# The last weight load cut into 16 loads of 8 partitions, and a new order of the last matmuls

## The chip, the core and the metric

The kernel runs on one core of a Trainium2 chip. The metric is the device time of one execution in microseconds; the median of the runs shown is what kernels are compared by. Engines: PE (TensorE) multiplies, DVE (VectorE) and ACT (ScalarE) do the elementwise work, SP (SyncE) issues the DMAs. All tensors are float32.

## What is computed

Two transformer blocks on 256 tokens of width 1024. Only the end matters here: the second block's mixture of experts and the final norm. Each of 16 experts takes 32 tokens (`cap`), chosen by the router:

```python
def expert(args):
    xe, wgu, wd = args
    gu = jnp.einsum('bcd,df->bcf', xe, wgu)
    ga, up = jnp.split(gu, 2, axis=-1)
    return jnp.einsum('bcf,fd->bcd', jax.nn.silu(ga) * up, wd)
ys = lax.map(expert, (jnp.swapaxes(xs, 0, 1), w_gu, w_down))
ys = jnp.swapaxes(ys, 0, 1) * gates[..., None].astype(ys.dtype)
return jax.vmap(lambda ib, yb: jnp.zeros((n, d), yb.dtype).at[ib.reshape(-1)].add(yb.reshape(-1, d)))(idx, ys)
...
x = x + ec_moe(rmsnorm_2(x, norm_ffn_g[layer]), router_w[layer], expert_w_gu[layer], expert_w_down[layer])
return rmsnorm_2(x, final_norm_g)
```

Each expert has weights of 1024x4096 (`w_gu`, 16 MB) and 2048x1024 (`w_down`, 8 MB): 384 MB in all, each byte used once.

## The kernel before, in words

`moe()` loops over the experts `e`. For one expert the `w_gu` load gives G and U (L1327), `silu(G)*U` is transposed to `aT` (L1359), `down` multiplies it by `w_down` (L1366 to L1371) and `scatter` (L1384 to L1394) copies the product out of PSUM and adds it, through a one-hot matrix with the gates in it (`ogT`), to four accumulators `acc[2*t + n]`: `t` is the half of the tokens, `n` the left or right 512 columns. Weights pass through large tiles named `eraw`; all loads are issued by SP, in program order.

The last expert (`e == 15`) is written out at L1416 to L1447. Its `w_down` comes in four parts `raws[0]` to `raws[3]` of 512 rows, four rows to a partition. Parts 0 to 2 are one load each (L1428, 2 MB). Part 3 comes as two loads of 1 MB, left columns and right columns (L1433), each over 128 partitions with four runs of 2 KB. The block under `self.strict()` (L1435 on) keeps PE, ACT and DVE in the written order: down left, scatter left, squares and gain of left; the same for right; then `rstd_q` (L257 to L272, a chain of small DVE and ACT steps on one column) turns the two sums of squares of each token half into a factor; then the scaling (L1445, L1446) and the two stores (L1447).

The order of DMAs on SP: each DMA from SP takes one of eight completion counters in turn (`DMAHW0` to `DMAHW7` in the listings below), so a DMA shares its counter with the one eight DMAs before it and, where that one isn't known to have landed, waits for it. SP issues in order: a DMA that waits holds back all behind it.

Of the kernel before, what the change touches and what calls it, by code (L numbers as in the profile page):

```python
# [9 lines left out]
F32 = mybir.dt.float32  # L10
# [3 lines left out]
AF = mybir.ActivationFunctionType  # L14
OP = mybir.AluOpType
# [4 lines left out]
D = 1024  # L20
# [12 lines left out]
class Body:  # L33
# [1177 lines left out]
    def moe(self):  # L1211
        tc, nc, a = self.tc, self.nc, self.a
        NE, CAP = 16, 32
        wgu, wdn = a["expert_w_gu_2"][0], a["expert_w_down_2"][0]
        with ExitStack() as es:
            ep, x = self.ep, self.x
            ewst = ExitStack()
            ew = self.open("ew", 1, ewst)
# [9 lines left out]
            def slot(n=4096):  # L1228
                pool, tag, bufs = slots[n_unit[0] % len(slots)]
                n_unit[0] += 1  # L1230
                return pool.tile([128, n], F32, name="eraw", tag=tag, bufs=bufs)
# [10 lines left out]
            for t in range(2):  # L1242
                l, r = self.logits[t][:, 0:NE], self.r4[t]
# [8 lines left out]
            p = self.ps()  # L1252
# [14 lines left out]
            p = self.ps()  # L1267
# [8 lines left out]
            acc = [self.ps("acc") for _ in range(4)]  # L1276
            for e in range(NE):
                q = e % 4
                wide = 4 <= e < NE - 1
                if e == 4:  # L1280
# [4 lines left out]
                    ew = self.open("ew4", 1, ewst)  # L1285
# [46 lines left out]
                p = self.ps()  # L1332
                for j in range(4):
                    for t in range(2):
                        nc.tensor.matmul(p[32 * j:32 * j + 32, 256:257], OH[:, t, e, :], self.rc[:, t:t + 1],  # L1335
                                         start=t == 0, stop=t == 1, tile_position=(0, 32 * j))
# [7 lines left out]
                ogT = ew.tile([128, 256], F32, name="ogT", tag="ogT")  # L1344
# [4 lines left out]
                p = self.ps()  # L1349
                if wide:  # L1350

                    idn = self.ident.rearrange("p (a b c) -> p a b c", a=2, b=2)
                    for i in range(8):
                        for b in range(2):
                            nc.tensor.matmul(p[64 * b:64 * b + 64, 64 * i:64 * i + 64], s[:, i:512:8], idn[:, :, b, :],  # L1355
                                             start=True, stop=True, tile_position=(0, 64 * b))
# [7 lines left out]
                y = {0: self.ps(), 512: self.ps()}  # L1364

                def down(j, raw, c0, n):  # L1366

                    for c in range(4):
                        o = 1024 * c + c0
                        nc.tensor.matmul(y[c0][32 * c:32 * c + 32, 0:n], aT[:, c, 32 * j:32 * j + 32],  # L1370
                                         raw[:, o:o + n], start=j == 0, stop=j == 3, tile_position=(0, 32 * c))  # L1371
# [8 lines left out]
                def rows(j):  # L1380
                    return wdn[e, 512 * j:512 * j + 512].rearrange("(p i) n -> p i n", i=4)


                def scatter(c0, n, out, first):  # L1384
                    ys = ew.tile([128, n], F32, name="ys", tag="ys")
                    if e == NE - 1 and c0:
                        nc.vector.tensor_copy(ys[:, 0:256], y[c0][:, 0:256])
                        nc.scalar.activation(ys[:, 256:512], y[c0][:, 256:512], AF.Copy)
                    elif c0 == 0:
                        nc.scalar.activation(ys, y[c0][:, 0:n], AF.Copy)  # L1390
                    else:
                        nc.vector.tensor_copy(ys, y[c0][:, 0:n])  # L1392
                    for t in range(2):
                        nc.tensor.matmul(out[t], ogT[:, t * 128:(t + 1) * 128], ys, start=first, stop=e == NE - 1)  # L1394

                if wide:
                    for j in range(2):
# [8 lines left out]
                if e < NE - 1:  # L1406
                    for n in range(2):
                        scatter(512 * n, 512, acc[n::2], e == 0)
                if e == 3:

                    for t in range(2):
                        for n in range(2):
                            nc.tensor.matmul(acc[2 * t + n], self.ident, x[:, t, 512 * n:512 * n + 512],  # L1413
                                             start=False, stop=False)

            end = e_[1][0].tile([128, 8192], F32, name="eraw", tag="e")  # L1416
            grow, g, junk = end[0:1, 0:D], end[:, D:2 * D], end[:, 2 * D:2 * D + 512]
            nc.sync.dma_start(grow, a["final_norm_g_2"].rearrange("(o d) -> o d", o=1))
            for n in range(2):
                p = self.ps()  # L1420
                nc.tensor.matmul(p, self.ones[0:1, :], grow[:, 512 * n:512 * n + 512], start=True, stop=True)
                nc.scalar.activation(g[:, 512 * n:512 * n + 512], p, AF.Copy)
            fo = end[:, 4 * D:6 * D].rearrange("p (t n) -> p t n", t=2)
            with self.queued([silu]):
                nc.scalar.activation(fo[:, 0, 0:1], self.eps, AF.Sqrt)
            raws = [w[:, o:o + 4096] for w in (slot(8192), slot(8192)) for o in (0, 4096)]
            for j in range(3):
                nc.sync.dma_start(raws[j], rows(j).rearrange("p i n -> p (i n)"))  # L1428
                for n in range(2):
                    down(j, raws[j], 512 * n, 512)  # L1430
            for n in range(2):
                c = slice(512 * n, 512 * n + 512)
                nc.sync.dma_start(raws[3].rearrange("p (i n) -> p i n", i=4)[:, :, c], rows(3)[:, :, c])  # L1433
            ss = [self.small.tile([128, 16], F32, name="ss", tag="st1", bufs=4) for _ in range(2)]
            with self.strict():  # L1435
                for n in range(2):
                    c = slice(512 * n, 512 * n + 512)
                    down(3, raws[3], 512 * n, 512)
                    scatter(512 * n, 512, acc[n::2], False)
                    for t in range(2):  # L1440
                        nc.scalar.activation(junk, acc[2 * t + n], AF.Square, accum_out=ss[t][:, n:n + 1])
                        nc.vector.tensor_tensor(fo[:, t, c], acc[2 * t + n], g[:, c], OP.mult)
                r = self.rstd_q(*ss)
                for t in range(2):
                    nc.scalar.activation(fo[:, t, 0:512], fo[:, t, 0:512], AF.Copy, scale=r[t])  # L1445
                    nc.vector.tensor_scalar(fo[:, t, 512:D], fo[:, t, 512:D], r[t], None, OP.mult)  # L1446
                    nc.sync.dma_start(self.out[t * 128:(t + 1) * 128, :], fo[:, t, :])  # L1447
            self.close(est, ewst, self.bigst)


# [44 lines left out]
```

## Time and profile before

| | us |
|---|---|
| median of 3 runs | 1509.54 |
| the runs | 1507.14, 1509.54, 1552.52 |
| the profiled execution, its own time | 1507.54 |
| its span, first to last instruction | 1505.8 |
| time outside the span | 1.7 |

In the page's 40 slices the DMA row stands at 9 from slice 19 on: over the experts the 16 DMA engines are the busy resource, and PE, at 6 tenths, waits for weights. In the last slices the loads run out and the chain passes to PE, ACT and DVE. Times in the timeline are microseconds from the start of the span; the number behind the start is the duration, and in square brackets stands how long the engine was idle before and what ended it.

### The profile page before, as it was taken

Reading aid. Unit: us, or ns where it says so; the run is one execution under the profiler, and the core shown is the slowest. Engines: PE = TensorE matmul, PEld = TensorE weight load, DVE = VectorE, ACT = ScalarE, POOL = GpSimd, SP = SyncE. Lnnn points to the kernel's source line nnn. Section 1 sums busy time; section 2 is a strip of 40 time slices with the busy share of each in tenths; the row PEclk is TensorE's granted clock in tenths of the full one; section 3 lists DMA queues with packets and bytes.
Section 4 is the critical chain, followed back from the end, with each engine's and each line's share of the span. In section 5 each row is a group of like instructions: output and inputs, shape, how many; then the busy total and the mean of one; then the engine's idle time right before and its main releaser. Section 6 shows DMA issues by size and latency. Waiting matters only on the chain.

```text
span 1505.8 us, 18173 instructions
## 1 busy us (share of the span) xinstructions
PE 1176.1 (78%) x7948; PEld 699.6 (46%) x7948; DVE 418.1 (28%) x786; ACT 356.7 (24%) x611; POOL 7.0 (0%) x19
## 2 busy tenths in 40 slices
PE   7999999999999999885676756666656666566665
PEld 5988989999978775321121211212211113112111
DVE  6844667455578855100000000000000000000001
ACT  5554556344466633000000000000000000000002
POOL 1000000000000000000000000000000000000000
PEclk9999999999999999998787788878878789778788
DMA  9754447555633289999999999999999999999995
GB/s 302 231 168 149 160 146 261 188 190 196 206 102 127 87 318 424 403 427 429 433 430 431 430 430 430 430 430 430 431 431 431 431 431 431 430 431 430 430 429 236
DMA packets 93054, 503.00 MB, mean 334 GB/s; under 512 B 7707, under 2 KB 60207, under 8 KB 78512
## 3 DMA queue, kind: packets, MB, share of 16 engines
q1 hardware_dynamic: 92976, 501.85, 82.8%
q8 instruction: 62, 1.02, 0.3%
q14 instruction: 16, 0.13, 0.0%
HBM read 500.79 MB, written 1.05 MB: 333 GB/s over the span
## 4 chain that ended last, share of the span: by engine, by line
PE 34%; another core or an unknown queue 15%; DMA 8%; DVE 2%; issue 1%; ACT 1%; SPq 0%; DVEq 0%; ACTq 0%
PE sm L1327 18%; DMA eraw<-in_expert_w_down_dram 8%; PE sm L1377 7%; PE acc L1394 4%; PE sm L1370 2%; PE sm L1355 2%; PE sm L1297 1%; DVE es L1348 1%; DVE ys L1392 1%; PE sm L1343 0%; ACT aT L1361 0%; PE acc L1413 0%; PE sm L1335 0%; DVE rsl L1338 0%
## 5 line engine op out<-in xcount | busy, mean ns | idle before, releaser
L1327 PE MATMUL sm<-eraw,xs 128*32 128x512 f32 x2048 | 318.5, 778 | 187.6 <-DMA eraw<-in_expert_w_gu_dram 187.6
L1327 PEld LDWEIGHTS sm<-eraw,xs 128*32 128x32 f32 x2048 | 75.0, 137 | 412.9 <-DMA eraw<-in_expert_w_gu_dram 211.3
L74 DVE TENSOR_TENSOR whl<-raw,whl 128x1024 fp32r<-128x1024 f32 x152 | 181.7, 1220 | 102.8 <-ACT whl L73 101.7
L73 ACT ACTIVATE whl<-raw 128x1024 fp32r<-128x1024 f32 x152 | 154.2, 1053 | 77.0 <-issue 46.0
L1377 PE MATMUL sm<-eraw,aT 128*32 128x512 f32 x704 | 106.5, 760 | 63.5 <-DMA eraw<-in_expert_w_down_dram 59.4
L1348 DVE SCALAR_TENSOR_TENSOR es<-sm,rsl,es 128x512 f32<-128x512 f32 x16 | 12.0, 750 | 443.6 <-PE sm L1327 440.7
L1347 ACT ACTIVATE es<-sm,rsl 128x512 f32<-128x512 f32 x16 | 11.0, 687 | 411.2 <-PE sm L1327 411.2
L127 PE MATMUL acc<-xh,whl 128*128 128x256 f32 x704 | 93.2, 280 | 0.0
L127 PE MATMUL sm<-xh,whl 128*128 128x256 f32 x704 | 89.7, 280 | 0.0
L1377 PEld LDWEIGHTS sm<-eraw,aT 128*32 128x32 f32 x704 | 26.1, 135 | 133.4 <-issue 62.8
L127 PEld LDWEIGHTS sm<-xh,whl 128*128 128x128 f32 x704 | 86.1, 189 | 0.7
L127 PEld LDWEIGHTS acc<-xh,whl 128*128 128x128 f32 x704 | 85.5, 188 | 1.1
L1392 DVE COPY ys<-sm 128x512 f32<-128x512 f32 x15 | 10.4, 691 | 236.5 <-PE acc L1394 236.5
L1394 PE MATMUL acc<-ys,ogT 128*128 128x512 f32 x128 | 64.3, 625 | 14.0 <-DVE ys L1392 11.9
L127 PE MATMUL acc<-whl,xh 128*128 128x512 f32 x240 | 65.4, 403 | 0.2
L1390 ACT ACTIVATE ys<-sm 128x512 f32<-128x512 f32 x16 | 9.6, 597 | 202.0 <-PE sm L1377 147.5
L1370 PE MATMUL sm<-eraw,aT 128*32 128x512 f32 x320 | 45.8, 710 | 13.8 <-DMA eraw<-in_expert_w_down_dram 10.7
L127 PE MATMUL acc<-whl,aH 128*128 128x512 f32 x176 | 55.7, 389 | 0.0
L1345 ACT ACTIVATE ogT<-sm 128x256 f32<-128x256 f32 x16 | 6.1, 383 | 195.2 <-PE sm L1343 195.2
L1394 PEld LDWEIGHTS acc<-ys,ogT 128*128 128x128 f32 x128 | 22.1, 193 | 58.8 <-issue 25.6
L127 PEld LDWEIGHTS acc<-whl,xh 128*128 128x128 f32 x240 | 44.4, 190 | 10.4 <-ACT xh L162 0.8
L127 PE MATMUL acc<-xl,whl 128*128 128x256 f32 x352 | 48.5, 278 | 0.0
(399 smaller groups left out, 1255.6 us busy)
## 6 DMA issues: line engine op xcount, KB each, us to landing
eraw<-in_expert_w_gu_dram SPq DMA_DIRECT2D x56, 4096.0 KB, 53.2
eraw<-in_expert_w_down_dram SPq DMA_DIRECT2D x22, 4096.0 KB, 53.0
eraw<-in_expert_w_down_dram SPq DMA_DIRECT2D x19, 2048.0 KB, 30.9
raw<-in_w_in_dram SPq DMA_DIRECT2D x34, 1024.0 KB, 5.4
eraw<-in_expert_w_gu_dram SPq DMA_DIRECT2D x16, 2048.0 KB, 17.3
raw<-in_w_gate_dram SPq DMA_DIRECT2D x11, 1024.0 KB, 5.4
raw<-in_w_up_dram SPq DMA_DIRECT2D x11, 1024.0 KB, 5.4
raw<-in_w_down_dram SPq DMA_DIRECT2D x11, 1024.0 KB, 4.9
```

What stands on the lines that cost most here:

```text
L73: nc.scalar.activation(H[:, k], raw[:, k], AF.Copy)
L74: self.at["L"] = nc.vector.tensor_tensor(L[:, k], raw[:, k], H[:, k].bitcast(F32), OP.subtract).ins
L127: nc.tensor.matmul(out, l[i], r[j], start=first and p == 0 and q == 0, stop=last and p == 2 and q == n - 1)
L1297: nc.tensor.matmul(pg[kk][:, i * 128:(i + 1) * 128], x[:, t, feats(k)], OH[:, t, e:e + 4, :].rearrange("p e s -> p (e s)"), start=t == 0, ...
L1327: nc.tensor.matmul(dst[32 * j:32 * j + 32, :], xs[:, k, 32 * q:32 * q + 32], raw[:, o + 512 * j:o + 512 * j + 512], start=k == 0, stop=k = ...
L1347: silu = nc.scalar.activation(s, G, AF.Silu, scale=rs).ins
L1348: nc.vector.scalar_tensor_tensor(s, U, rs, s, OP.mult, OP.mult)
L1355: nc.tensor.matmul(p[64 * b:64 * b + 64, 64 * i:64 * i + 64], s[:, i:512:8], idn[:, :, b, :], start=True, stop=True, tile_position=(0, 64 ...
L1370: nc.tensor.matmul(y[c0][32 * c:32 * c + 32, 0:n], aT[:, c, 32 * j:32 * j + 32], raw[:, o:o + n], start=j == 0, stop=j == 3, tile_position ...
L1377: nc.tensor.matmul(y[c0][32 * c:32 * c + 32, :], aT[:, i, j, :], raw[:, o:o + 512], start=j == 0 and i < 4, stop=j == 1 and i >= 4, tile_p ...
L1392: nc.vector.tensor_copy(ys, y[c0][:, 0:n])
L1394: nc.tensor.matmul(out[t], ogT[:, t * 128:(t + 1) * 128], ys, start=first, stop=e == NE - 1)
```

## The change

`raws[3]`'s right half is loaded by 16 DMAs of 8 partitions each instead of one of 128. The right columns of `down` become two groups of 256 columns, at 512 and at 768, in two PSUM banks, for all four parts. In the last block `down` of both halves stands ahead of the left scatter; the right half is copied out of PSUM by DVE (columns 512 on) and ACT (768 on) into `yr`, and its scatter is two matmuls of 256 columns for each token half. The gain of the last accumulator (`acc[3]`) is no longer a step of its own: it is done with the factor in one instruction at the end. Both stores are outside the strict block.

```diff
                 def scatter(c0, n, out, first):
                     ys = ew.tile([128, n], F32, name="ys", tag="ys")
-                    if e == NE - 1 and c0:
-                        nc.vector.tensor_copy(ys[:, 0:256], y[c0][:, 0:256])
-                        nc.scalar.activation(ys[:, 256:512], y[c0][:, 256:512], AF.Copy)
-                    elif c0 == 0:
+                    if c0 == 0:
                         nc.scalar.activation(ys, y[c0][:, 0:n], AF.Copy)
                     else:
                         nc.vector.tensor_copy(ys, y[c0][:, 0:n])
                     for t in range(2):
-                        nc.tensor.matmul(out[t], ogT[:, t * 128:(t + 1) * 128], ys, start=first, stop=e == NE - 1)
+                        nc.tensor.matmul(out[t], ogT[:, t * 128:(t + 1) * 128], ys, start=first, stop=False)
...
+            y[768] = self.ps()
             for j in range(3):
                 nc.sync.dma_start(raws[j], rows(j).rearrange("p i n -> p (i n)"))
-                for n in range(2):
-                    down(j, raws[j], 512 * n, 512)
+                for c0, n in ((0, 512), (512, 256), (768, 256)):
+                    down(j, raws[j], c0, n)
             for n in range(2):
                 c = slice(512 * n, 512 * n + 512)
-                nc.sync.dma_start(raws[3].rearrange("p (i n) -> p i n", i=4)[:, :, c], rows(3)[:, :, c])
+
+                for o in range(0, 128, 8) if n else (0,):
+                    i = slice(o, o + (8 if n else 128))
+                    nc.sync.dma_start(raws[3].rearrange("p (i n) -> p i n", i=4)[i, :, c], rows(3)[i, :, c])
             ss = [self.small.tile([128, 16], F32, name="ss", tag="st1", bufs=4) for _ in range(2)]
             with self.strict():
+                down(3, raws[3], 0, 512)
+                yl = ew.tile([128, 512], F32, name="ys", tag="ys")
+                nc.scalar.activation(yl, y[0], AF.Copy)
+                for c0 in (512, 768):
+                    down(3, raws[3], c0, 256)
+                yr = ew.tile([128, 2, 256], F32, name="yr", tag="es")
+                nc.vector.tensor_copy(yr[:, 0], y[512][:, 0:256])
+                for t in range(2):
+                    nc.tensor.matmul(acc[2 * t], ogT[:, t * 128:(t + 1) * 128], yl, start=False, stop=True)
+                nc.scalar.activation(yr[:, 1], y[768][:, 0:256], AF.Copy)
                 for n in range(2):
-                    c = slice(512 * n, 512 * n + 512)
-                    down(3, raws[3], 512 * n, 512)
-                    scatter(512 * n, 512, acc[n::2], False)
                     for t in range(2):
+                        if n:
+                            for i in range(2):
+                                nc.tensor.matmul(acc[2 * t + 1][:, 256 * i:256 * i + 256], ogT[:, t * 128:(t + 1) * 128],
+                                                 yr[:, i], start=False, stop=i == 1)
                         nc.scalar.activation(junk, acc[2 * t + n], AF.Square, accum_out=ss[t][:, n:n + 1])
-                        nc.vector.tensor_tensor(fo[:, t, c], acc[2 * t + n], g[:, c], OP.mult)
+                        if n == 0:
+                            nc.vector.tensor_tensor(fo[:, t, 0:512], acc[2 * t], g[:, 0:512], OP.mult)
+                nc.vector.tensor_tensor(fo[:, 0, 512:D], acc[1], g[:, 512:D], OP.mult)
                 r = self.rstd_q(*ss)
                 for t in range(2):
                     nc.scalar.activation(fo[:, t, 0:512], fo[:, t, 0:512], AF.Copy, scale=r[t])
-                    nc.vector.tensor_scalar(fo[:, t, 512:D], fo[:, t, 512:D], r[t], None, OP.mult)
-                    nc.sync.dma_start(self.out[t * 128:(t + 1) * 128, :], fo[:, t, :])
+                nc.vector.tensor_scalar(fo[:, 0, 512:D], fo[:, 0, 512:D], r[0], None, OP.mult)
+                nc.vector.scalar_tensor_tensor(fo[:, 1, 512:D], acc[3], r[1], g[:, 512:D], OP.mult, OP.mult)
+            for t in range(2):
+                nc.sync.dma_start(self.out[t * 128:(t + 1) * 128, :], fo[:, t, :])
```

SP's queue at the end of the program, before. The names in brackets are what the DMA waits for; `DMAHW` is a counter of an earlier DMA.

```order
L1236 DMA eraw<-in_expert_w_gu_dram 128x8192 [waits DMAHW4_49,PE_49]
L1418 DMA eraw<-in_final_norm_g_dram 1x1024 [waits DMAHW7_49,PE_49]
L1428 DMA eraw<-in_expert_w_down_dram 128x4096 [waits DMAHW5_49]
L1428 DMA eraw<-in_expert_w_down_dram 128x4096
L1428 DMA eraw<-in_expert_w_down_dram 128x4096 [waits DMAHW6_49]
L1433 DMA eraw<-in_expert_w_down_dram 128x4x512
L1433 DMA eraw<-in_expert_w_down_dram 128x4x512 [waits DMAHW0_49]
L1447 DMA out_dram<-eraw 128x1024 [waits DMAHW1_49,DVE_49,Activation_49]
L1447 DMA out_dram<-eraw 128x1024 [waits DMAHW2_49,DVE_49,Activation_49]
```

The same place in the changed kernel, from the left half on; of the 16 small loads the counters run from 0 to 7 twice.

```order
L1434 DMA eraw<-in_expert_w_down_dram 128x4x512
L1434 DMA eraw<-in_expert_w_down_dram 8x4x512 [waits DMAHW0_49]
L1434 DMA eraw<-in_expert_w_down_dram 8x4x512 [waits DMAHW1_49]
...
L1434 DMA eraw<-in_expert_w_down_dram 8x4x512 [waits DMAHW6_49]
L1434 DMA eraw<-in_expert_w_down_dram 8x4x512 [waits DMAHW7_49]
L1434 DMA eraw<-in_expert_w_down_dram 8x4x512 [waits DMAHW0_49]
...
L1434 DMA eraw<-in_expert_w_down_dram 8x4x512 [waits DMAHW6_49]
L1434 DMA eraw<-in_expert_w_down_dram 8x4x512 [waits DMAHW7_49]
L1463 DMA out_dram<-eraw 128x1024 [waits DMAHW0_49,DVE_49,Activation_49]
L1463 DMA out_dram<-eraw 128x1024 [waits DMAHW1_49,DVE_49,Activation_49]
```

One load that waited on counter 0 has become 16 that wait on counters 0 to 7 and again 0 to 7. Counter 7 is the left half's; the stores' counters moved from 1 and 2 to 0 and 1.

PE at the end of the program, before (`ys` is the copy of the product, `acc` the accumulators):

```order
L1370 MATMUL sm<-eraw,aT 32x512 [waits DMAHW7_49]
L1370 MATMUL sm<-eraw,aT 32x512 x3
L1394 MATMUL acc<-ys,ogT 128x512 [waits Activation_49]
L1394 MATMUL acc<-ys,ogT 128x512
L1370 MATMUL sm<-eraw,aT 32x512 [waits DMAHW0_49]
L1370 MATMUL sm<-eraw,aT 32x512 x3
```

and the same in the changed kernel:

```order
L1370 MATMUL sm<-eraw,aT 32x512 [waits DMAHW7_49]
L1370 MATMUL sm<-eraw,aT 32x512 x3
L1370 MATMUL sm<-eraw,aT 32x256 [waits DMAHW4_49,DMAHW5_49,DMAHW3_49,DMAHW6_49,DMAHW2_49,DMAHW7_49,DMAHW1_49,DMAHW0_49]
L1370 MATMUL sm<-eraw,aT 32x256 x7
L1445 MATMUL acc<-ys,ogT 128x512 [waits Activation_49]
L1445 MATMUL acc<-ys,ogT 128x512
L1451 MATMUL acc<-yr,ogT 128x256 [waits DVE_49]
L1451 MATMUL acc<-yr,ogT 128x256 [waits Activation_49]
```

The left scatter (L1394, now L1445) stood between the two halves of `down` and now stands behind both, so behind the first matmul of the right half, which waits on all eight counters.

## Rows read from the trace of the kernel before

**Rows 1.** The page's slices: DMA engines' share in tenths, GB/s.

```profile
DMA  9754447555633289999999999999999999999995
GB/s 302 231 168 149 160 146 261 188 190 196 206 102 127 87 318 424 403 427 429 433 430 431 430 430 430 430 430 430 431 431 431 431 431 431 430 431 430 430 429 236
```

**Rows 2.** Timeline, last expert: start, duration, engine, line, operation, idle before.

```profile
1461.58 5.34 PE L1327 MATMUL sm<-eraw,xs 128*32 128x512 f32 x32 [4.16 <-DMA eraw<-in_expert_w_gu_dram]
...
1471.32 6.07 PE L1327 MATMUL sm<-eraw,xs 128*32 128x512 f32 x32 [4.40 <-DMA eraw<-in_expert_w_gu_dram]
...
1477.52 0.75 DVE L1348 SCALAR_TENSOR_TENSOR es<-sm,rsl,es 128x512 f32<-128x512 f32 x1 [31.27 <-PE sm L1327]
...
1486.09 1.92 PE L1370 MATMUL sm<-eraw,aT 128*32 128x512 f32 x16 [1.54 <-DMA eraw<-in_expert_w_down_dram]
...
1488.77 1.06 PE L1370 MATMUL sm<-eraw,aT 128*32 128x512 f32 x8 [0.75 <-DMA eraw<-in_expert_w_down_dram]
...
1490.61 1.98 PE L1394 MATMUL acc<-ys,ogT 128*128 128x512 f32 x4 [0.78 <-ACT ys L1390]
...
1492.52 1.07 PE L1370 MATMUL sm<-eraw,aT 128*32 128x512 f32 x8
...
1494.90 1.98 PE L1394 MATMUL acc<-ys,ogT 128*128 128x512 f32 x4 [1.31 <-ACT ys L1388]
...
1496.98 0.60 ACT L1441 ACTIVATE eraw<-acc 128x512 f32<-128x512 f32 x1 [0.23 <-PE acc L1394]
...
1497.48 0.19 ACT L1441 ACTIVATION_READ_ACCUMULATOR eraw<-acc 128x1 f32 x1
...
1498.31 0.20 DVE L264 TENSOR_SCALAR rstq<-ss 128x1 f32<-128x1 f32 x1
...
1500.06 0.21 DVE L271 TENSOR_SCALAR rstq<-rstq 128x1 f32<-128x1 f32 x1
...
1500.19 0.87 DVE L1446 TENSOR_SCALAR eraw<-eraw,rstq 128x512 f32<-128x512 f32 x2
```

**Rows 3.** The two loads of part 3: issue durations and starts, time to landing.

```profile
L1433 SPq DMA_DIRECT2D eraw<-in_expert_w_down_dram x2: 603/4726/8850, 1447.8 to 1451.8; - x2
...
DMA to landing us min/median/max: 39.5/40.2/40.9
```

**Rows 4.** SP's waits from 1440 us on.

```profile
SPq L1433 <- DMA eraw<-in_expert_w_gu_dram: 3.4, 1, 3.4
```

**Rows 5.** Issues of small loads on SP, by timeline and by line.

```profile
4.12 5.09 SPq L390 DMA_DIRECT2D bf<-in_b_forget_dram  x1
...
408.45 0.36 SPq L759 DMA_DIRECT2D cw<-in_mlstm_conv_w_dram  x1
...
1445.92 0.24 SPq L1418 DMA_DIRECT2D eraw<-in_final_norm_g_dram  x1
...
L771 SPq DMA_DIRECT2D pw<-in_pool_w_dram x4: 486/586/596, 410.8 to 414.0; - x4
...
DMA to landing us min/median/max: 1.9/2.0/3.6
```

**Rows 6.** Busy time by stretch; the last three columns are PEclk, DMA share, GB/s.

```profile
1476.00:1484.00 8.00, 7.06 (x52) 2.28 (x44) 0.75 (x1) 3.96 (x6) 0.00 (x0) 0.98 1.01 412
...
1485.00:1489.00 4.00, 2.15 (x20) 0.57 (x24) 0.00 (x0) 0.00 (x0) 0.00 (x0) 1.00 0.50 186
...
1442.23:1445.87 3.64, 3.64 (x48) 1.41 (x48) 0.00 (x0) 0.00 (x0) 0.00 (x0) 1.00 1.00 428
...
1461.58:1466.92 5.34, 5.34 (x32) 1.26 (x32) 0.00 (x0) 0.00 (x0) 0.00 (x0) 0.68 1.02 436
...
1489.80:1497.00 7.20, 5.00 (x20) 1.51 (x16) 1.93 (x4) 3.06 (x9) 0.00 (x0) 1.00 0.05 20
```

**Rows 7.** DMA packets of the stretch 1485 to 1489.

```profile
q1 hardware_dynamic: 382, 0.74, 49.6%
```

## The prediction

> **What bounds the kernel now.** I read the page's slices first, then the timeline of the last 65 us, then the DMA issues of that stretch. The slices show the DMA engines full from slice 19 on at about 430 GB/s [rows 1]: 384 MB of expert weights set the time, and nothing in the change touches that part. What it can touch is the end, behind the last weight byte.
>
> There the reader is to see three moments. The left half of part 3 was issued at 1447.8 and took 40.9 us to land, so 1488.7; PE starts on it at 1488.77 [rows 2, 3]. The right half was issued at 1451.8 and took 39.5, so 1491.3 [rows 3]. PE starts on it at 1492.52, with no idle time in the row, because it was still at the left scatter, 1490.61 to 1492.59 [rows 2]. So the right half's landing is not on the path: it has 1.2 us to spare. From 1492.52 to the end of the span at 1505.8 are 13.28 us: right down 1.07, a wait for the copies, scatter 1.98 from 1494.90, squares, the factor chain, scaling, stores.
>
> Before 1484 the 16 DMA engines are at share 1.01, from 1485 at 0.50 [rows 6]: half of them have run out of work some 6 us ahead of the others. That is the slack that a different split of the last megabyte could use.
>
> **The change, part by part, against the profiled execution: 1507.54 us, span 1505.8.** That is 2.0 under the median shown (1509.54), and 0.4 above the lowest run.
>
> *The new order behind the landing.* Call t0 the moment at which PE can start the right half's matmuls. Behind it now stand, in PE's order: right down 1.07 (two groups of 256 columns for one of 512, the same columns), left scatter 1.98, right scatter 1.98 [rows 2]; together 5.03. The two copies of the right product lie beside the left scatter now and cost nothing; the cover is 1.98 us of PE, the copies need under 0.5 each. ACT's last square ended 0.79 behind PE's last scatter (1494.90 + 1.98 = 1496.88 to 1497.67): 5.82. DVE's gain of the last accumulator has left this place. The factor chain took from 1498.31 to 1500.27, 1.96 us, of which its first column's steps can start before the last square is done, so that it ends at about t0 + 7.6. The scaling took 0.79 from there to 1501.06 [rows 2]; one of its two instructions (about 0.48, the overlap of the pair taken out) is now a scalar_tensor_tensor that reads PSUM, 0.75 by its row, so 1.06: t0 + 8.7. From there to the end 4.74 as before (1501.06 to 1505.8). Sum: t0 + 13.4, against 13.28 before. The reordering, seen from the right half's start, is worth nothing: what it takes out (waiting copies, one gain) is what it puts in (the left scatter, 1.98, which was done beforehand). It pays only if t0 comes earlier than 1492.52.
>
> *The extra matmuls of parts 0 to 2.* Same columns, twelve more instructions; PE idles 1.54 and 0.75 before the next parts [rows 2], which covers them. Nothing.
>
> *The 16 loads, and what t0 becomes.* The second load of part 3 waited 3.4 us for a w_gu load [rows 4], and 8.85 us more in its issue [rows 3]: that w_gu load is eight DMAs ahead of it, and the listing shows the wait on counter 0. The 16 loads wait in the same way, each for the DMA eight before it. The first seven wait for loads that are needed earlier anyhow (the third w_gu load was there at 1461.58, the last at 1471.32, part 2 at 1486.09 [rows 2]) and are out by then. **The eighth waits on counter 7, and that is the left half, which lands at 1488.7.** SP issues in order, so loads 8 to 16, 9/16 of the right half, cannot be issued before 1488.77, whatever DMA engines stand idle. Load 16 needs counter 7 again: load 8's landing.
>
> The price of such an issue and landing is not in the trace for this shape. Nearest rows: 0.24 (one partition), 0.36 (20 partitions), 0.49 to 0.60 (64 partitions, 16 KB) for an issue, 1.9 to 2.0 for the landing of a small load, 3.6 at worst [rows 5]. I take 0.36 for the issue, whose row is nearest in partitions, 0.05 between two, and 2.0 for the landing. Load 16 is issued eight slots behind load 8: 1488.77 + 8 x 0.41 = 1492.05, and has landed at 1494.05. Load 8 itself lands at 1490.8, so load 16 isn't held by it. So t0 = 1494.05, 1.5 later than PE starts on the right half now, and 4.2 us later than PE is ready for it (1488.77 + 1.06). Ends: 0.24 with 0.04 between and a landing of 1.9 give 1492.9; 0.60 with 0.05 and 2.0 give 1496.0.
>
> *PE's clock in the new gap.* [...] In the trace the 32 matmuls behind a gap of 4.16 took 5.34 us at a mean clock of 0.68, those behind 4.40 took 6.07, and the same kind of work with PE busy ran at 1.00 (3.64 us in the stretch from 1442.23) [rows 2, 6]. So a gap like this cost 1.7 and 2.4; gaps of 1.5 cost nothing. I take 1.7, from the row with the nearest gap; the ends are 0 and 2.4. All of PE's 5.03 us behind t0 is on the path, so it counts in full.
>
> **Sum:** t0 later by 1.5, the tail by 0.1, the clock 1.7: +3.3 to +3.4 us. 1507.54 + 3.4 = **1510.9 us**. Low end of this case: 0.4 + 0.1 = +0.5; high end: 3.5 + 0.1 + 2.4 = +6.0.
>
> **Rivals.**
>
> *A. The balance works.* The 16 loads land by the time the left half's matmuls end (1489.84), because they sit on DMA engines that run out at about 1485. Then t0 = 1489.84, no gap, the end at 1489.84 + 13.4 = 1503.2: 2.6 us less, 1504.9. For it: the share of 0.50 from 1485 on, and 64 packets to an engine are only 64 x 0.083 = 5.3 us (382 packets in 4 us at 49.6% of 16 engines are 83 ns each [rows 7]), which fits between about 1482 and 1489. Against it: the wait on counter 7 in SP's queue, which no faster engine lifts. [...] Chance 0.15.
>
> *B. The issue is dear.* The only load over 8 partitions in the trace, L390, held SP for 5.09 us [rows 5]. At that price the nine late loads take 9 x 5.1 = 46 us, t0 is about 1537 and the kernel 44 us slower, 1552: over 2%. It decides from about 3.5 us an issue on. Against it: L390 reads single elements and is issued 4 us after the start, when SP is just filling the queue, and larger loads there take 0.4 to 0.8; the right half's own 8.85 [rows 3] came with some 15 MB of loads still ahead of it, and at 1489 none is. Chance 0.03.
>
> *C. The clock stays up, or the issues are at the cheap end.* +0.5 to +1.7, 1508.0 to 1509.2. This is the low part of the forecast's range; it shares its 0.70.
>
> The remaining 0.12 is for holds that are shorter than computed and land between A and C, 1505 to 1508.
>
> **How the numbers follow.** Forecast 0.70 (with C), A 0.15, B 0.03, the rest 0.12. The time is the likeliest case's, 1510.9. The range reaches down to A, 1504.9, with 0.4 for the spread to the lowest run, and up to 1507.54 + 6.0 = 1513.5 with 2.0 for the distance of the profiled execution to the median: 1504.5 to 1515.5. A measurement of this kernel can tell about 2%, 30 us, from no change. Only B reaches that: slower 0.03; no mechanism here gains 30 us, faster 0.01; within 2% 0.96.
>
> **What would show it.** In the profile of the changed kernel: the left half's matmuls start near 1488.8 as now; SP's issues of the small loads show seven spread out over 1452 to 1486 and nine in a row from 1488.8 on, at 0.3 to 0.6 each; PE idles about 4 us between the left and the right half of part 3 and names a w_down DMA for it; its clock in the last 12 us is under 1.00; from the right half's start to the end of the span are 13.4 us at full clock, 15 otherwise. Wrong would be: small loads issued in a row before 1488, an idle time of PE there under 1 us (rival A), or single issues of several us after 1488 (rival B). If the tail is 13.4 but t0 is off, the issue price or the landing was mis-sized; if t0 is right and the tail long, the clock.

## The result, and the profile after

| | before | after |
|---|---|---|
| median, us | 1508.76 (4 runs) | 1517.61 (1516.58 to 1517.95, 4 runs) |
| the profiled execution, its span | 1507.54, 1505.8 | 1517.95, 1515.9 |

The ratio is 1.0059, interval 1.0048 to 1.0071: slower by 0.6%, about 9 us, outside the forecast range (1504.5 to 1515.5) on the side that was forecast. One of the runs of before, at 1552.52, was disturbed and is left out of the ratio.

The chain of waits of the changed kernel, from the left half's issue on (start, duration, what):

```profile
1448.72 41.95 DMA eraw<-in_expert_w_down_dram
1490.67 0.02 issue
1490.68 0.67 SPq L1434
1491.36 0.04 issue
1491.40 0.67 SPq L1434
...
1495.69 0.67 SPq L1434
1496.36 0.04 issue
1496.41 4.58 DMA eraw<-in_expert_w_down_dram
1500.99 0.14 issue
1501.13 1.93 PE sm L1370 x16
```

The left half lands at 1490.67, SP issues the eighth small load in the same moment, seven more behind it 0.72 apart, and the last one at 1496.41; that one takes 4.58 us to land. The SPq pieces are the chain: this is the hold on counter 7 that the prediction named. SP's own rows agree. It waits four times for w_down loads, 15.1 us in all. The last of these waits runs from the end of the seventh small load's issue, 1488.55, to the left half's landing. Below: the waits, the seventh issue, and the issues of part 3 (left half and 16 loads: shortest, median and longest issue).

```profile
SPq L1434 <- DMA eraw<-in_expert_w_down_dram: 15.1, 4, 5.7
```

```profile
1487.88 0.67 SPq L1434 DMA_DIRECT2D eraw<-in_expert_w_down_dram  x1
```

```profile
L1434 SPq DMA_DIRECT2D eraw<-in_expert_w_down_dram x17: 613/672/9092, 1448.7 to 1496.4; - x17
```

The timeline of the changed kernel, to be held against [rows 2]:

```profile
1471.70 5.22 PE L1327 MATMUL sm<-eraw,xs 128*32 128x512 f32 x32 [4.76 <-DMA eraw<-in_expert_w_gu_dram]
...
1487.91 4.48 PE L1370 MATMUL sm<-eraw,aT 128*32 128x512 f32 x32 [3.81 <-DMA eraw<-in_expert_w_down_dram]
...
1501.13 1.93 PE L1370 MATMUL sm<-eraw,aT 128*32 128x256 f32 x16 [8.73 <-DMA eraw<-in_expert_w_down_dram]
...
1502.99 3.29 PE L1445 MATMUL acc<-ys,ogT 128*128 128x512 f32 x4
...
1506.12 1.89 PE L1451 MATMUL acc<-yr,ogT 128*128 128x256 f32 x8
...
1510.84 0.75 DVE L1461 SCALAR_TENSOR_TENSOR eraw<-acc,rstq,eraw 128x512 f32<-128x512 f32 x1
```

PE idles 8.73 us ahead of the right half, where 4.2 were forecast, and the left scatter behind it takes 3.29 instead of 1.98. Also part 2 and the left half come later: PE waits 3.81 us for part 2, where it waited 1.54.

Busy time by stretch of the changed kernel (last three columns PEclk, DMA share, GB/s):

```profile
1482.00:1485.00 3.00, 2.10 (x32) 0.77 (x24) 0.00 (x0) 0.00 (x0) 0.00 (x0) 1.00 0.90 277
...
1495.00:1500.00 5.00, 0.00 (x0) 0.00 (x0) 0.00 (x0) 0.00 (x0) 0.00 (x0) 0.54 0.48 66
...
1501.13:1508.01 6.88, 6.88 (x28) 3.35 (x28) 1.85 (x4) 2.45 (x7) 0.00 (x0) 0.67 0.00 0
```

```profile
q1 hardware_dynamic: 207, 0.33, 48.0%
```

The second fence is the DMA packets of 1495 to 1500. The DMA share is 0.48 there and the traffic 66 GB/s; in the kernel before about the same share moved 186 [rows 6]. A packet took 0.48 x 16 x 5 / 207 = 0.185 us, against 0.083 in [rows 7].

At 1482 to 1485 the first small loads run beside parts 2 and 3. There the whole core's traffic is down too, to 277 GB/s. The same stretch of the kernel before:

```profile
1482.00:1485.00 3.00, 2.55 (x24) 0.52 (x16) 0.00 (x0) 0.00 (x0) 0.00 (x0) 1.00 0.97 380
```

Packets of 16 KB belong here to parts 0 to 2 alone. Taken one by one from the trace, they last 0.80 us in the mean in this stretch, 0.64 before. So something slowed the small loads' packets and those of other loads with them. The prediction had no term for that.

### The profile page after: what moved, and what is told of

It reads as the page before. It is cut to its first block, busy times and chain, and to the rows that moved or that the text cites. A ratio compares the mean times of both kernels' runs of the same rounds, so it can differ in the third digit from the quotient of the medians.

```text
span 1515.9 us, 18266 instructions
## 1 busy us (share of the span) xinstructions
PE 1183.0 (78%) x7984; PEld 703.1 (46%) x7984; DVE 417.9 (28%) x785; ACT 356.6 (24%) x611; POOL 7.0 (0%) x19
## 4 chain that ended last, share of the span: by engine, by line
PE 71%; another core or an unknown queue 14%; DMA 9%; DVE 3%; ACT 2%; issue 1%; SPq 1%; DVEq 0%; ACTq 0%
PE acc L127 20%; PE sm L1327 18%; PE sm L127 10%; DMA eraw<-in_expert_w_down_dram 8%; PE sm L1377 7%; PE acc L1391 3%; PE sm L1370 2%; PE sm L1355 2%; PE sm L1297 1%; PE acc L1176 1%; DVE es L1348 1%; DVE ys L1389 1%; PE acc L1208 1%; DMA x<-in_x_dram 0%
## 5 line engine op out<-in xcount | busy, mean ns | idle before, releaser
L1377 PE MATMUL sm<-eraw,aT 128*32 128x512 f32 x704 | 111.9, 794 | 57.9 <-DMA eraw<-in_expert_w_down_dram 54.9
L1391 PE MATMUL acc<-ys,ogT 128*128 128x512 f32 x120 | 59.5, 618 | 11.9 <-DVE ys L1389 11.9
L1370 PE MATMUL sm<-eraw,aT 128*32 128x512 f32 (+1 forms) x352 | 45.7, 664 | 24.9 <-DMA eraw<-in_expert_w_down_dram 22.0
L127 PE MATMUL sm<-xl,whl 128*128 128x256 f32 x352 | 48.3, 280 | 0.0
```

What stands on the lines that cost most here:

```text
L127: nc.tensor.matmul(out, l[i], r[j], start=first and p == 0 and q == 0, stop=last and p == 2 and q == n - 1)
L1377: nc.tensor.matmul(y[c0][32 * c:32 * c + 32, :], aT[:, i, j, :], raw[:, o:o + 512], start=j == 0 and i < 4, stop=j == 1 and i >= 4, tile_p ...
```

## The experiments

Two theories were to be told apart. *Hold*: the small loads that are issued only behind the left half's landing, times the price of an issue, make the loss. *Place*: loads that cover few neighbouring partitions are slow and slow the others. Since kernels reach the end some 1 to 3 us earlier or later for reasons far ahead of it, the table counts from PE's start on the last w_gu load (W), where PE waits for its landing in every kernel.

| right half | W | left half start | right half start | span | right half from W | from there to the end |
|---|---|---|---|---|---|---|
| before: 1 load, old order | 1471.32 | 1488.77 | 1492.52 | 1505.8 | 21.2 | 13.3 |
| after: 16 x 8 neighbours | 1471.70 | (landed 1490.67) | 1501.13 | 1515.9 | 29.4 | 14.8 |
| E1: 1 load, new order | 1470.80 | in one row with part 2 | 1490.84 | 1503.6 | 20.0 | 12.8 |
| E2: 7 loads, neighbours | 1471.00 | 1491.23 | 1494.49 | 1510.0 | 23.5 | 15.5 |
| E3: 8 x 16 neighbours | 1472.74 | in one row with part 2 | 1496.50 | 1510.8 | 23.8 | 14.3 |
| E4: 16 x 8, four apart | 1470.89 | 1488.26 | 1496.62 | 1510.8 | 25.7 | 14.2 |
| E5: 16 x 8 neighbours, old order | 1473.26 | 1492.27 | 1501.47 | 1517.0 | 28.2 | 15.5 |
| E6: 7 loads, eight apart | 1471.08 | 1490.27 | 1494.32 | 1509.5 | 23.2 | 15.2 |
| E7: 16 loads of 128 x 512 B | 1473.67 | in one row with part 2 | 1496.02 (last wait) | 1510.4 | 22.4 | 14.4 |
| E8: 4 x 32, four apart | 1474.19 | 1491.56 | 1494.32 | 1506.9 | 20.1 | 12.6 |
| E9: 4 x 32 neighbours | 1473.10 | 1495.00 | 1497.88 | 1512.0 | 24.8 | 14.1 |

All but E5 have the new order of the matmuls. `i` are the partitions of a load. Each kernel was profiled once. From W to the end the profiles differ from before's 34.5 us as the ratios of the run times do, within 1.8 us (the changed kernel 9.7 more against 8.9, E4 5.4 against 5.9). So a few tenths between two rows of the table are not shown to be real.

### E1: the order alone

```diff
-                for o in range(0, 128, 8) if n else (0,):
-                    i = slice(o, o + (8 if n else 128))
+                for i in (slice(0, 128),):
```

> The new order of the last matmuls with the right half in one load of 128 partitions as before. If the loss is all in the 16 loads: the right half lands near 1491.4 us, PE idles about 1.5 us between the halves of part 3 with its clock at the upper level, and the end comes 13.4 us after that start: span about 1504.9, 1 us under before, ratio 0.999 to 1.000. If the order itself costs (left scatter behind the right half, one more wait): span 1507 or more.

Measured: 1507.09 us, ratio 0.9985 (0.9975 to 0.9994), span 1503.6: 0.15% faster than before, and the only kernel here whose interval lies below 1.

```profile
1490.84 1.07 PE L1370 MATMUL sm<-eraw,aT 128*32 128x256 f32 x16 [0.67 <-DMA eraw<-in_expert_w_down_dram]
1491.84 1.98 PE L1444 MATMUL acc<-ys,ogT 128*128 128x512 f32 x4
1493.66 1.89 PE L1450 MATMUL acc<-yr,ogT 128*128 128x256 f32 x8
```

PE goes through right half and both scatters without a gap, at a granted clock of 1.00 from 1490.84 to 1495.55; the copies lie beside the left scatter. The order gains 1.2 us up to the right half's start and 0.5 behind it. All of the loss is in the 16 loads.

### E5: the loads alone

```diff
-                nc.sync.dma_start(raws[3].rearrange("p (i n) -> p i n", i=4)[:, :, c], rows(3)[:, :, c])
+                for i in [slice(o, o + 8) for o in range(0, 128, 8)] if n else (slice(0, 128),):
+                    nc.sync.dma_start(raws[3].rearrange("p (i n) -> p i n", i=4)[i, :, c], rows(3)[i, :, c])
```

> The kernel before with the 16 loads of 8 neighbouring partitions for the right half and nothing else changed. If the landing sets the end, the old order gives back nothing: the left scatter runs at 1490.6 as before, PE then waits for the right half until about 1501, and from there 13.3 us at full clock, 14.5 to 15 behind the long gap: span 1514.5 to 1516, ratio about 1.005, the changed kernel's. If the new order were a part of the loss: 2 us or more under the changed kernel.

Measured: 1518.91 us, ratio 1.0059 (1.0044 to 1.0074), span 1517.0. From W to the end 43.7 us against 44.2 in the changed kernel, and both have the ratio 1.0059: as expected, the loads alone make the whole loss. The new order's gain of 1.7 us (E1) is gone once the late landing sets the end; the changed kernel, which has that order, is even 0.5 longer from W. The span is 1 us over the expected one, since W is 1.6 later.

### E4: the same 16 loads, their partitions four apart

```diff
-                for o in range(0, 128, 8) if n else (0,):
-                    i = slice(o, o + (8 if n else 128))
+                for i in [slice(32 * b + r, 32 * b + 32, 4) for b in range(4) for r in range(4)] if n else (slice(0, 128),):
```

> The changed kernel with its 16 loads of 8 partitions, each load's partitions four apart instead of neighbours; the counters, the waits, the issues and the bytes are the same. If packets are slow because eight of them go to neighbouring partitions: packets near 87 ns to the end (207 ns in the changed kernel after 1495), no slowdown at 1482 to 1485, left half landed at 1489 instead of 1490.7, last landing about 2.5 us after its issue: PE starts on the right half near 1497, span near 1512, 4 us less. [...]

Measured: 1515.43 us, ratio 1.0039 (1.0025 to 1.0053), span 1510.8. That span is 5 us under the changed kernel's, but the profiled run is the fastest of E4's five; by the ratios the gain is 0.2%, 3 us, and from W to the end it is 4.3. Timeline and two stretches of E4, then the packets of the second stretch:

```profile
1488.26 1.06 PE L1370 MATMUL sm<-eraw,aT 128*32 128x512 f32 x8 [0.72 <-DMA eraw<-in_expert_w_down_dram]
1496.62 1.94 PE L1370 MATMUL sm<-eraw,aT 128*32 128x256 f32 x16 [7.30 <-DMA eraw<-in_expert_w_down_dram]
```

```profile
1482.00:1485.00 3.00, 2.26 (x36) 0.83 (x28) 0.00 (x0) 0.00 (x0) 0.00 (x0) 1.00 0.66 262
...
1490.00:1495.00 5.00, 0.00 (x0) 0.00 (x0) 0.00 (x0) 0.05 (x1) 0.00 (x0) 0.81 0.31 92
```

```profile
q1 hardware_dynamic: 280, 0.46, 31.5%
```

A packet took 0.315 x 16 x 5 / 280 = 0.090 us, near the 0.083 of before, and half of the changed kernel's 0.185 (the expectation's 207 ns is 185 by that row). At 1482 to 1485 a share of 0.66 moved 262 GB/s, where the changed kernel needed 0.90 for 277. The left half came in time, and the right half 3.7 us earlier from W (25.7 against 29.4). The 92 GB/s of the second stretch are what SP issues: 64 KB each 0.72 us. Same loads, same counters, same issues: place costs 3.7 us in these two profiles. What is left, 25.7 against E1's 20.0, is hold: the left half's matmuls start at 1488.26, the right half's 8.4 us behind, while eight issue slots and one landing of 2.5 us go by.

### E7: 16 loads over all partitions

```diff
-                for o in range(0, 128, 8) if n else (0,):
-                    i = slice(o, o + (8 if n else 128))
-                    nc.sync.dma_start(raws[3].rearrange("p (i n) -> p i n", i=4)[i, :, c], rows(3)[i, :, c])
+                for q in [(r, slice(c.start + o, c.start + o + 128)) for r in range(4) for o in range(0, 512, 128)] if n else ((slice(0, 4), c),):
+                    nc.sync.dma_start(raws[3].rearrange("p (i n) -> p i n", i=4)[:, q[0], q[1]], rows(3)[:, q[0], q[1]])
```

> The changed kernel with its 16 loads cut the other way: each over all 128 partitions, one run of 512 B in each (64 KB as before), on the same counters, so that loads 8 to 16 still wait for the left half. Hold theory: nine issues in a row behind 1488.2, each 0.4 (as a load with one run per partition) to 0.7 (as now), landing 2 to 2.5 us behind the last: PE starts on the right half at 1493.7 to 1496.5, span 1507.5 to 1511, 3 to 6 us over the new order with one load, though no packet is slowed by neighbours. If only neighbouring partitions cost: as the new order with one load, 1503.5 to 1505.

Measured: 1511.0 us, ratio 1.0012 (1.0002 to 1.0022), span 1510.4, last wait for the right half over at 22.4 from W. The line of its loads and their time to landing, then its chain from the left half's landing on:

```profile
L1433 SPq DMA_DIRECT2D eraw<-in_expert_w_down_dram x17: 328/431/8164, 1450.3 to 1494.7; - x17
...
DMA to landing us min/median/max: 1.9/2.1/40.7
```

```profile
1491.04 0.02 issue
1491.05 0.33 SPq L1433
...
1493.80 2.09 DMA eraw<-in_expert_w_down_dram
1495.89 0.14 issue
1496.02 1.88 PE sm L1370 x10
```

The hold is there though these loads land 2.1 us behind their issue at the median: SP issues the eighth load when the left half has landed, 1491.05. Each of these loads brings 128 columns of one row to every partition, so PE starts on the right half before all have landed; the wait that ends last is for the load issued at 1493.80, six slots behind the eighth, and ten of the sixteen matmuls follow it. That wait ends 22.4 from W, E1's 20.0, so 2.4 us of hold. From W to the end E7 takes 3.9 us more than E1, within the 3 to 6 expected; the left scatter is in that (2.93 us against E1's 1.98, in a stretch with a granted clock of 0.75). The rest of the span's distance from E1 is W, 2.9 later. An issue of one run per partition costs 0.43 at the median where one of four runs costs 0.67. So the price of the hold is the slots that PE has to wait for, eight here at most, times the issue's price, and that price goes with the pattern more than with the partitions: 128 partitions with one run are cheaper than 8 with four.

### E2 and E3: 7 and 8 loads of neighbours

From here on a diff shows the new line alone; it stands in place of the same two lines as in E4.

```diff
+                for i in [slice(o, o + 16) for o in range(0, 96, 16)] + [slice(96, 128)] if n else (slice(0, 128),):
```

> New order, right half in 7 loads (six of 16 partitions, one of 32), so that no load waits for the left half's counter. If the hold on counter 7 is what costs: SP shows no wait after 1487, the right half lands near 1491.5 and the span is about 1505. If many small loads are slow in themselves (packets longer than 87 ns where a load covers few partitions): the landing is 1493 to 1496 and the span 1507 to 1510, with no wait on SP.

Measured: 1511.47 us, ratio 1.0018 (1.0006 to 1.003), span 1510.0; SP waits for part 2 at the last load, not for the left half. Right half 23.5 from W and not 20: without any load held by the left half the loads cost 3.5 us. The left half itself starts 2.8 late (1491.23, 20.2 from W against 17.4), which no hold explains. That spoke for place. For the right half it proves less, since the last load is held too, by part 2, and stands in the chain:

```profile
1487.80 6.56 DMA eraw<-in_expert_w_down_dram
```

```diff
+                for i in [slice(o, o + 16) for o in range(0, 128, 16)] if n else (slice(0, 128),):
```

> New order, right half in 8 loads of 16 partitions: the eighth alone waits for the left half's counter. Hold theory: its issue starts when the left half has landed (1489), takes 0.65, lands 2 to 4 us later, PE starts on the right half at 1492 to 1493.5, span 1505.5 to 1508, 1 to 2 us more than with 7 loads. If the hold is nothing: the same as with 7 loads.

Measured: 1512.85 us, ratio 1.0023 (1.0014 to 1.0032), span 1510.8, right half 23.8 from W: 0.3 more than with 7 loads. That does not price one held load, because both kernels have one in their chain: here the eighth is issued when the left half has landed (1492.70) and takes 3.64 us to land, in E2 the seventh waits for part 2.

```profile
1492.72 3.64 DMA eraw<-in_expert_w_down_dram
```

As a test of the hold this pair was too weak, and place stood over it.

### E6: 7 loads, eight apart

```diff
+                for i in [slice(o, 128, 8) for o in (0, 1, 2, 4, 5, 6)] + [slice(3, 128, 4)] if n else (slice(0, 128),):
```

> The kernel with 7 loads (six of 16 partitions, one of 32), with the partitions of each load eight or four apart instead of neighbours; no load waits for the left half. Neighbour theory: packets stay near 87 ns, the left half lands at 1488 as with one load (1491.2 with 7 loads of neighbours), PE starts on the right half at 1490.8 to 1491.8 instead of 1494.5, span 1503.5 to 1505, the same as the new order with one load. If it is the number of loads that makes them slow: 1494 and 1509 to 1510 as with neighbours.

Measured: 1511.61 us, ratio 1.0016 (1.0007 to 1.0026), span 1509.5, right half 23.2 from W: a miss. "Neighbours" was the wrong word for it. The stretch in which the small loads begin, E6 first, then E2:

```profile
1482.00:1485.00 3.00, 2.18 (x36) 0.78 (x24) 0.00 (x0) 0.00 (x0) 0.00 (x0) 1.00 0.97 208
```

```profile
1482.00:1485.00 3.00, 3.00 (x24) 0.98 (x20) 0.00 (x0) 0.47 (x1) 0.00 (x0) 0.50 1.00 231
```

All 16 DMA engines are busy (share 0.97 and 1.00) at 208 and 231 GB/s; the kernel before moved 380 in the same stretch at 0.97. (The last load of these seven waits for part 2 as in E2, so a part of the 3.2 us over E1 may be that hold.) So partitions eight apart kept the core's traffic down as neighbours did, though part 2 and the left half run in this stretch as well; E4's partitions, four apart, had moved 262 GB/s there at a share of 0.66. The next two runs differ in the distance alone.

### E8 and E9: 4 loads of 32, four apart and neighbours

```diff
+                for i in [slice(o, 128, 4) for o in range(4)] if n else (slice(0, 128),):
```

> [...] If a load of few partitions is slow however they lie (7 loads eight apart were, with about 208 GB/s at 1482 to 1485): 1493 to 1495, span 1507 or more.

Measured: 1507.8 us, ratio 0.9993 (0.9984 to 1.0003), span 1506.9 at a W that is 3.4 later than E1's: right half 20.1 from W, and 12.6 from there to the end, both within 0.2 of E1. (The 1493 to 1495 of the expectation is PE's start on the right half. It was 1494.32, within that range only because W is late: counted from E1's W it is 1490.9.)

```diff
+                for i in [slice(o, o + 32) for o in range(0, 128, 32)] if n else (slice(0, 128),):
```

> [...] If 32 partitions are enough for any split: as with partitions four apart.

Measured: 1513.29 us, ratio 1.0032 (1.002 to 1.0044), span 1512.0. The stretch of the small loads in E8, then in E9:

```profile
1484.00:1487.00 3.00, 2.69 (x44) 1.10 (x36) 0.00 (x0) 0.00 (x0) 0.00 (x0) 1.00 1.03 408
```

```profile
1484.00:1488.00 4.00, 1.61 (x24) 0.52 (x16) 0.00 (x0) 0.00 (x0) 0.00 (x0) 1.00 1.01 222
```

The left half's matmuls in E8's timeline, then in E9's:

```profile
1491.56 1.06 PE L1370 MATMUL sm<-eraw,aT 128*32 128x512 f32 x8 [0.73 <-DMA eraw<-in_expert_w_down_dram]
```

```profile
1495.00 1.07 PE L1370 MATMUL sm<-eraw,aT 128*32 128x512 f32 x8 [0.72 <-DMA eraw<-in_expert_w_down_dram]
```

The DMA packets of the two stretches, E8 and E9:

```profile
q1 hardware_dynamic: 362, 1.22, 102.7%
```

```profile
q1 hardware_dynamic: 274, 0.89, 101.5%
```

Four loads in both, their issues over by 1481.0 in E8 and 1480.1 in E9, where PE gets part 2 at 1488.91 and 1490.70, so no hold by part 2 or the left half in either: 408 against 222 GB/s with all engines busy (share 1.03 and 1.01), and 4.7 us at the right half's start. This settles that place costs. The left half, not itself a small load, starts 4.5 us later from W in E9 than in E8 (21.9 against 17.4): the small loads hold up the packets of others. A packet lasts 0.237 us in the mean in E9's stretch (1.015 x 16 x 4 / 274) and 0.136 in E8's (1.027 x 16 x 3 / 362); in both a tenth of the packets are of 8 KB or more.

Why place costs is not shown. A step of four partitions was harmless (E4: 0.090 us a packet; E8: 408 GB/s), one of eight was not (E6: 208 GB/s), nor were neighbours (E2: 231, E9: 222). The number of partitions in a load does not sort them: 8 were harmless in E4, 32 were not in E9. E4's small loads alone kept 0.31 of the DMA engines busy between 1490 and 1495; how many engines E9's loads use at once no row shows apart from part 2's, so whether the engines have a part in it stays open. Moving the partitions also moves the rows that are read in DRAM; no run here separates the two ends.

## Why the prediction was wrong, point by point

The mechanism that it had was right: the hold on counter 7, the nine issues behind it, PE's gap, the slower clock behind the gap. A second one, the slowing by place, it left out. What failed is the step "The price of such an issue and landing is not in the trace for this shape", with its 0.36 and 2.0, and with it the sentence that t0 would be at most 1496.0. t0 was 1501.13, 7.1 later than forecast:

- *The left half's landing*, taken as 1488.77, was 1490.67: 0.4 from a later W, 1.5 because the first small loads held up the core's traffic. No term stood for that. E4 shows it: the same loads four apart leave the left half at 17.4 from W, as before.
- *The issue*, taken as 0.36 + 0.05 by the row of 20 partitions, was 0.67 + 0.04: 8 x 0.72 = 5.7 instead of 3.3, 2.5 more. The row to take was L1433's own 0.603 [rows 3]: the same pattern of four runs, on more partitions. E7 shows that the pattern sets the price: 0.43 for one run on 128 partitions.
- *The landing*, taken as 2.0, was 4.58: 2.6 more. With the partitions four apart the last load landed about 2.5 us behind its issue (E4: eight slots of 0.72 from 1488.2, then PE's start at 1496.62). So again place. The row that the 2.0 came from, L771, covers 64 partitions.

The sum: 0.4 + 1.5 + 2.5 + 2.6 and the 0.14 from landing to PE's start are the 7.1.

*The tail* was forecast at 13.4 at full clock plus 1.7 and measured 14.8. At full clock it is 12.8 and 12.6 (E1, E8): in E1 PE's three groups take 4.71 us together where 5.03 were added up, and the factor chain ends 7.2 behind their start instead of 7.6. *The clock* cost 2.2, within the bounds given: the same matmuls take 6.88 us at 0.67 behind the gap of 8.73, and 4.71 behind E1's gap of 0.67. Both in E1's rows, the last step of the factor chain and the stretch of PE's three groups:

```profile
1497.86 0.21 DVE L271 TENSOR_SCALAR rstq<-rstq 128x1 f32<-128x1 f32 x1
```

```profile
1490.84:1495.55 4.71, 4.71 (x28) 2.61 (x28) 1.85 (x4) 2.51 (x8) 0.00 (x0) 1.00 0.00 0
```

*The reordering is worth nothing behind the right half's start*: nearly, 0.5 us; with a t0 that comes earlier it pays, as the text had it, and E1 is that case.

*Rival A*, the balance: refuted by SP's wait, which held the eighth load until 1490.67. Its 64 packets to an engine take it that the small loads keep to half of the engines; no run shows this by engine, only a share of 0.48 at 1495 to 1500. And its 83 ns a packet were 0.185 us there. *Rival B*, issues of 5 us: refuted, 0.67. *Rival C*: refuted, since the clock fell to 0.67 behind the gap and the issue was dearer than the forecast's 0.36.

## What to carry to other kernels

Count the DMAs that stand behind the last big load. Where counters are given out eight in turn, as here, the eighth shares one with it, and all from there on are issued only when it has landed, one whole issue after the other (here from 1490.67 on, 0.72 us apart). Choose the pieces of a load by where their partitions lie: cut by every fourth partition (E4: 0.090 us a packet; E8: 408 GB/s), or by runs over all partitions (E7: landings of 2.1 us at the median), the pieces were slowed little or not at all; cut by neighbours (E2: 231 GB/s, E9: 222, the changed kernel: 277) or by every eighth (E6: 208), they slowed themselves and the transfers beside them (the left half came 19.0 to 21.9 us from W, 17.4 in E4 and E8). For an issue's price take the row with the same access pattern (0.60 [rows 3], where 0.67 came), not with the nearest number of partitions (0.36).

## What the runs showed of the hardware that was not expected

- Small loads at 8 neighbouring partitions: 66 GB/s and 0.185 us a packet; the same four apart: 0.090 us.
- With all DMA engines busy and part 2 still running, 32 neighbours a load 222 GB/s and 0.237 us a packet in the mean, 32 partitions four apart 408 and 0.136.
- An SP issue of four runs per partition 0.67 us for 8 partitions and 0.60 for 128 [rows 3]; of one run, 0.43 for 128.
- Why the share of the DMA engines falls from 1.01 before 1484 to 0.50 from 1485 on [rows 6], some 6 us ahead of the last landing, stays open, and so does which of them are idle. E8, with four loads that wait for nothing late, gains nothing clear over E1's one load (ratio 0.9993 against 0.9985), so it is open too what a split that uses the idle share could gain.
